# Two-layer encoder trunk on one core: another order of the transfers and small steps in the Fourier part that opens the kernel

## The chip, the cores and the metric

One Trainium2 chip, and one of its cores. The metric is the device time of one execution in microseconds (us), taken as the median of several runs; less is better. The profile describes one further execution, recorded by the hardware profiler.

## The reference, cut to what matters

Two inputs of 512 tokens by 1024 features, a prompt and a sample, go through the same two layers. Layer 0 mixes tokens with a two-dimensional Fourier transform, layer 1 with attention, and each is followed by a squared-ReLU MLP. All arithmetic is f32.

```python
def fourier_mix(h, w_out):
    B, S, _ = h.shape
    hg = h.astype(jnp.float32).reshape(B, S, N_FGROUPS, F_GROUP)
    f = jnp.fft.fft2(hg, axes=(1, 3), norm="ortho").real
    f = f.reshape(B, S, D_MODEL).astype(h.dtype)
    return f @ w_out
...
        if i % N_MIXERS == 0:
            x = x + fourier_mix(rms_norm(x, fourier_norm[j]), fourier_w_out[j])
        else:
            x = x + gqa_attention(rms_norm(x, attn_norm[j]), ...)
        x = x + sq_relu_mlp(rms_norm(x, mlp_norm[i]), mlp_w_up[i], mlp_w_down[i])
    return rms_norm(x, final_norm)
```

The features fall into 8 groups of 128, so the transform along the features is a product with a 128 by 128 table, and the one along the tokens a product with a 512 by 512 table.

## The kernel before, in words

The change touches only the Fourier part, which is about the first 6% of the span. It stands in one block under a manual schedule (L795 and after): each engine runs its instructions in the order in which the code issues them, so a step that waits holds up everything that the code puts behind it on that engine. TensorE is PE, VectorE DVE, ScalarE ACT, GpSimd POOL; SyncE (SP) only starts transfers.

**Sequences and tiles.** Sequence 0 is the prompt, sequence 1 the sample. Each has four tiles of 128 tokens. A `Front` object prepares two tiles of a sequence: `f0` and `f1` for sequence 0, `g0` and `g1` for sequence 1. It squares them on ACT (L130), forms the reciprocal root in six small steps (`chain`, L141 to L146, the second on ACT, the others on DVE), applies the gain (L429), and folds the 1024 features to their sum (`plus`, L433) and difference (`minus`, L442). For sequence 1 the sum is not made on DVE: `plus_there` (L438) has POOL start a transfer that adds one half of the tile onto the other while it is written (an accumulating transfer). `combine` (L464 to L489) joins the two tiles, `scale` (L453) brings them to the same root, and for sequence 1 the halves are split into two fp32r parts, high on ACT and low on DVE (L86, L87, L499, L504).

**The first product** is `transform_exact` (L643 to L668) for sequence 0: exact_even (L529), exact_odd (L532), exact_nyq (L535), then the feature products (L564, L585, L586). PE fills its waits there with a few idle products (`idle`, L604). Its results are split on ACT and DVE (L86, L87).

**The weights** of the output product are folded the same way by four `Fold` objects: `minus` (L684) makes the difference on DVE and then has POOL add the other half of the weight onto the first by an accumulating transfer (L685); odd_hi (L690) and even_hi (L702) are the high parts on ACT, odd_lo (L694) and even_lo (L705) the low parts on DVE.

**The second product** multiplies by these weights: eight odd outputs into the eight PSUM banks at once (`odd_outs`, L739), then the even ones (`even_outs`), each three products per part (L81, L82, L83) and one for the Nyquist rows (L745), whose weights POOL fetches (`FoldNyq.fetch`, L727). `odd_put` (L768, L769) and `even_put` (L777, L779) carry the banks to SBUF on ACT, which frees them. The residual input is added to the result by accumulating transfers of POOL (`add_input`, L792, one for each of the four tiles xs[0,0] to xs[0,3], 512 KB each), and the even part by two more on POOL for tiles 0 and 1 (`add_even`, L784) and on DVE for tiles 2 and 3 (L787, L789).

**Sequence 1** follows in `transform(1)` (L618 to L641): products with tables that POOL loads (dcos, dsin, dalt, dfeat; `table`, L329), evacuated by the splits of L86 and L87 one pair of banks after another. A hook called between them squares the finished tiles of sequence 0 for the next norm (`square`, L178 on ACT, then an addition on POOL, L182). Then `even_outs(1)` begins, and among its outputs stands the root of sequence 0 (`root`, L191, two columns per tile on PE), which reads the sum that POOL's last addition leaves. After it comes the spread of the root (L199), and the first MLP with its products (L1029).

**Loads.** SP starts the x tiles (L319), `load_xs(1)` (L168: the four residual tiles of sequence 1, 512 KB each), `put_away` (L212: a finished tile goes to DRAM, `park`), and the first MLP weights (`load_raw`, L101, 512 KB each). PSUM has 8 banks, each reused in order of the code; SBUF tiles of one kind share 38 slots, so a load can wait for a slot.

Of the kernel before, what the change touches and what calls it, by code (L numbers as in the profile page):

```python
# [16 lines left out]
ALU = mybir.AluOpType  # L17
# [27 lines left out]
def trunk_kernel(ctx, tc, x_in, xt_in, y_out, tables, rope, gfour, gcol, grow, gfin,  # L45
# [277 lines left out]
    def put_nyq():  # L323
        nyqs.append(slot([P, 512], F32R))
        nc.scalar.copy(nyqs[0], exact[2][:, 334:846])

    def table(k):
        tabs[k] = slot([P, D], F32R)
        nc.gpsimd.dma_start(tabs[k][:, : tables[k].shape[-1]], tables[k])  # L329
# [60 lines left out]
    def eights(x, n):  # L390
        return x[:, 0:512:64].unsqueeze(1).broadcast_to([P, n, 8])
# [14 lines left out]
    class Front:  # L406
# [52 lines left out]
        def low(self, i):  # L459
# [2 lines left out]
            nc.scalar.copy(self.n[i][:, :, 0], eights(self.m[i], 2))  # L462
            parts.append((self.p[i], self.m[i], self.n[i]))

        def combine(self):
            (p1, p2), (m1, m2), r, w = self.p, self.m, self.r, 8
            stt = nc.vector.scalar_tensor_tensor
            if self.q == 0:
                n, = nyq_tiles(1)
                stt(n[:, :, 0], eights(m2, 2), r[:, 1:2], eights(m1, 2), ALU.mult, ALU.add)  # L470
                stt(m2, m2, r[:, 1:2], m1, ALU.mult, ALU.subtract)
# [56 lines left out]
    def exact_even(k, j, o):  # L528
        nc.tensor.matmul(o[:, :258], parts[k][0][:, j * P : (j + 1) * P], cosX[k], start=k == 0, stop=k == 2)  # L529

    def exact_odd(k, j, v):
        nc.tensor.matmul(v[:, :256], parts[k][1][:, j * P : (j + 1) * P], sinX[k], start=k == 0, stop=k == 2)  # L532
# [67 lines left out]
    def idle(o, n, zero=None):  # L600

        w, alone = (filler, True) if zero is None else (zero, False)
        for _ in range(n):
            nc.tensor.matmul(o[:, :256], w, filler.unsqueeze(1).broadcast_to([P, 2, P]), start=alone, stop=alone)  # L604
# [35 lines left out]
        nyq_out(q, en)  # L640
        hook("feat", 3)  # L641

    def transform_exact(mid, hook):  # L643
        ov = [(ps(), ps()) for _ in range(4)]
        for k in range(2):
            for j in range(4):
                exact_even(k, j, ov[j][0])
            for j in range(4):
                exact_odd(k, j, ov[j][1])
        idle(ov[3][1], 9, an[:, :P])  # L650
        mid()
        ab = []
        for j in range(4):
            exact_odd(2, j, ov[j][1])
            exact_even(2, j, ov[j][0])
            ab.append(seq_evac(0, *ov[j]))
            hook("seq", j)
        on = ps()
        for k in range(3):
            exact_nyq(k, on)  # L660
        put_an(on)
        put_low(on)
        hook("an", 0)
        o = [feat_exact(*ab[j]) for j in range(2)]
        for j in range(4):
            feat_nyq(o[j][0], j)
            feat_split(0, j, *o[j])
            hook("feat", j)  # L668
            if 0 < j < 3:
                o.append(feat_exact(*ab[j + 1]))  # L670
# [80 lines left out]
    def odd_outs(q, fos):  # L751
        return outs(q, fos, wo, 256, 256)
# [42 lines left out]
    with tc.manual_schedule(engines={ET.PE, ET.Activation, ET.DVE, ET.Pool, ET.SP}):  # L795
# [29 lines left out]
        f0.root(1, 3, 4)  # L825
        f0.minus(1)
        f0.root(1, 4, 6)
        f0.table(1)
        f1.squares(1)
        f1.chain(1, 2)  # L830
        f0.low(0)
        f0.low(1)
        ftX = exact[2][:, :256]
        f1.gain(0)
        f1.minus(0)
        f1.gain(1)
        sums3 = []

        def mid():
            f1.chain(0, 1)  # L840
            f1.chain(2, 3)
            f1.plus(0)
            f1.chain(3, 4)
            f1.minus(1)
            f1.chain(4, 6)
            f1.scale()
            put_nyq()
            f1.plus(1)
            f1.combine()
            sums3.extend(odd_sums(k) for k in range(3))  # L850

        def hook0(at, j):
            if at == "seq":
                if j == 1:
                    for k in range(3):
                        put_sums(k, sums3[k])
                elif j == 3:
                    for f in fold:
                        f.minus()
                    fold[0].odd_hi()  # L860
            elif at == "an":
                fold[0].odd_lo()
# [11 lines left out]
        transform_exact(mid, hook0)  # L874
# [12 lines left out]
        g0.minus(0)  # L887
        g0.plus_there(0)
        for j in range(4):
            fold[j].even_hi()  # L890
        g0.chain(3, 4)
        fold[0].even_lo()
        g0.chain(4, 5)
        fold[1].even_lo()
        g0.chain(5, 6)
        fold[2].even_lo()
        fold[3].even_lo()
        for fo in range(2):
            odd_put(0, fo, o[fo])
        add_input(0, 0)  # L900
        g0.scale(slice(0, 1))
        for fo in range(2, 4):
            odd_put(0, fo, o[fo])
        add_input(0, 1)
# [10 lines left out]
        g1.squares(1)  # L915
        g1.chain(1, 2)
        for fo in range(6, 8):
            odd_put(0, fo, o[fo])
        g1.gain(1)
        g1.minus(1)  # L920
        g1.plus_there(1)
        for i in range(2, 4):
            add_input(0, i)

        def even(fo):
            even_put(0, fo, even_outs(0, [fo])[0])

        for fo in range(3):
            even(fo)
        g0.combine()  # L930
        g1.chain(0, 1)
        g1.chain(2, 3)
        add_even(0, 0)
        g0.split_even()
        g1.chain(3, 4)
        g0.split_odd()
        g1.chain(4, 6)
        even(3)
        g1.scale(slice(0, 1))
        g1.scale(slice(1, 2))  # L940
# [12 lines left out]
        blocks = Blocks(0)  # L953

        def hook1(at, j):
            if at == "seq":
                if j < 3:
                    square(0, j)
            else:
                square(0, 3 + j)  # L960
                if j == 3:
                    square(0, 7)

        transform(1, hook1)
        for fo in range(KC):
# [1244 lines left out]
```

## Time and profile before

| what | value |
|---|---|
| median of 3 runs | 1677.88 us (1676.66 to 1679.09) |
| the profiled execution's own time | 1676.81 us |
| its span in the trace | 1675.0 us, so 1.81 us lie around it |
| PE busy | 1662.4 us, 99% of the span |
| DVE, ACT, POOL busy | 76%, 52%, 23% |
| waits of PE listed with a releaser | 5.7 us in all, longest 1.2 us |
| the root of sequence 0 on PE (L191) begins | 74.06 us |

Times in a timeline count from the span's start. A row gives the start, the duration, the engine, the line, the operation and the tiles (result first), and in square brackets how long the engine stood idle before it and which event ended that. In a waits row stand the engine and its line, the event that it waited for, and then the us in total, the number of waits and the longest. A windows row gives for a stretch the busy time of PE, PE's weight loads, DVE, ACT and POOL, each with its count of instructions, then PE's granted clock, the mean busy share of the 16 DMA engines, and what they moved in GB/s.

### The profile page before, as it was taken

Reading aid. Unit: us, or ns where it says so; the run is one execution under the profiler, and the core shown is the slowest. Engines: PE = TensorE matmul, PEld = TensorE weight load, DVE = VectorE, ACT = ScalarE, POOL = GpSimd, SP = SyncE. Lnnn points to the kernel's source line nnn. Section 1 sums busy time; section 2 is a strip of 40 time slices with the busy share of each in tenths; the row PEclk is TensorE's granted clock in tenths of the full one; section 3 lists DMA queues with packets and bytes.
Section 4 is the critical chain, followed back from the end, with each engine's and each line's share of the span. In section 5 each row is a group of like instructions: output and inputs, shape, how many; then the busy total and the mean of one; then the engine's idle time right before and its main releaser. Section 6 shows DMA issues by size and latency. Waiting matters only on the chain.

```text
span 1675.0 us, 22279 instructions
## 1 busy us (share of the span) xinstructions
PE 1662.4 (99%) x7828; PEld 1386.3 (83%) x7828; DVE 1264.7 (76%) x1855; ACT 872.8 (52%) x1546; POOL 391.5 (23%) x370
## 2 busy tenths in 40 slices
PE   9999999999999999999999999999999999999998
PEld 8888888888888888888888888888888888888887
DVE  8679786557886869869888877777855487878875
ACT  7766444446343425446688855554454562433334
POOL 3321443221000001324444303004422220000002
PEclk9999999999999999999999999999999999999999
DMA  9942655449775757425501156334544695757632
GB/s 327 259 151 95 210 185 196 158 164 362 266 226 159 244 176 238 164 82 183 174 9 38 64 175 222 119 120 169 208 146 167 222 377 188 232 157 227 187 102 101
DMA packets 122480, 303.53 MB, mean 181 GB/s; under 512 B 12376, under 2 KB 13528, under 8 KB 122368
## 3 DMA queue, kind: packets, MB, share of 16 engines
q1 hardware_dynamic: 98720, 253.53, 43.7%
q0 software_dynamic: 9248, 22.10, 6.3%
q10 hardware_dynamic: 14400, 26.48, 4.2%
q8 instruction: 61, 1.00, 0.2%
q14 instruction: 51, 0.42, 0.1%
HBM read 217.59 MB, written 82.38 MB: 179 GB/s over the span
## 4 chain that ended last, share of the span: by engine, by line
PE 94%; DVE 2%; DMA 2%; ACT 1%; issue 0%; POOL 0%; SPq 0%; DVEq 0%; ACTq 0%; POOLq 0%
PE ps L1029 74%; PE ps L83 6%; PE ps L82 6%; PE ps L81 6%; PE ps L1624 2%; DMA u<-u 1%; DMA u<-spill_b 1%; PE ps L1603 0%; PE ps L191 0%; ACT u L86 0%; DVE u L429 0%; DMA u<-spill_t 0%; ACT w L702 0%; DVE u L87 0%; DVE t L442 0%
## 5 line engine op out<-in xcount | busy, mean ns | idle before, releaser
L1029 PE MATMUL ps<-u,w 128*128 128x512 f32 x4944 | 1131.0, 389 | 0.0
L1029 PEld LDWEIGHTS ps<-u,w 128*128 128x128 f32 x4944 | 926.4, 188 | 195.0 <-ACT u L1062 1.7
L86 ACT CAST w<-raw 128x1024 fp32r<-128x1024 f32 (+1 forms) x216 | 213.5, 994 | 309.8 <-PE ps L1029 238.4
L87 DVE TENSOR_TENSOR w<-raw,w 128x1024 fp32r<-128x1024 f32 (+1 forms) x216 | 251.4, 1167 | 75.4 <-ACT w L86 75.2
L86 ACT CAST u<-u 128x1024 fp32r<-128x1024 f32 (+1 forms) x140 | 140.7, 1046 | 85.3 <-PE ps L1029 37.9
L87 DVE TENSOR_TENSOR u<-u,u 128x1024 fp32r<-128x1024 f32 (+1 forms) x140 | 168.7, 1232 | 19.6 <-ACT u L86 19.1
L1029 PE MATMUL ps<-u,u 128*128 128x512 f32 x600 | 143.4, 389 | 0.5 <-DVE t L1239 0.5
L1239 DVE TENSOR_TENSOR u<-ps,u 128x512 f32<-128x512 f32 x160 | 109.4, 685 | 37.8 <-PE ps L1029 34.5
L1266 POOL DMA_DIRECT2D raw<-w_sum x32 | 27.7, 866 | 469.6 <-DVE w L87 164.7
L1147 POOL TENSOR_TENSOR u<-u 128x512 f32<-128x512 f32 x28 | 37.7, 1346 | 424.4 <-ACT u L1044 424.4
L1029 PEld LDWEIGHTS ps<-u,u 128*128 128x128 f32 x600 | 112.5, 188 | 24.6 <-DVE t L1239 0.9
L81 PE MATMUL ps<-u,u 128*128 128x512 f32 (+2 forms) x340 | 128.7, 381 | 1.2 <-ACT u L777 1.1
L82 PE MATMUL ps<-u,u 128*128 128x512 f32 (+2 forms) x340 | 124.1, 366 | 0.9 <-DVE u L87 0.9
L83 PE MATMUL ps<-u,u 128*128 128x512 f32 (+2 forms) x340 | 124.1, 366 | 0.2 <-DVE u L87 0.2
L182 POOL TENSOR_TENSOR t<-t,t 128x512 f32<-128x512 f32 (+1 forms) x54 | 79.2, 1471 | 191.9 <-ACT t L178 190.7
L1043 ACT ACTIVATE t<-t 128x512 f32<-128x512 f32 x64 | 40.5, 632 | 109.9 <-DVE t L1116 99.9
L83 PEld LDWEIGHTS ps<-u,u 128*128 128x128 f32 x340 | 64.2, 189 | 11.1 <-DVE u L87 0.7
L82 PEld LDWEIGHTS ps<-u,u 128*128 128x128 f32 x340 | 64.4, 189 | 10.3 <-DVE u L87 2.2
L87 DVE TENSOR_TENSOR u<-ps,u 128x512 fp32r<-128x512 f32 (+3 forms) x112 | 68.0, 634 | 6.3 <-ACT u L86 5.8
L81 PEld LDWEIGHTS ps<-u,u 128*128 128x128 f32 x340 | 64.4, 189 | 9.5 <-ACT u L777 1.4
L1103 DVE TENSOR_TENSOR t<-ps,u 128x512 f32<-128x512 f32 x32 | 22.0, 687 | 60.4 <-PE ps L1029 52.6
L178 ACT ACTIVATE t<-u 128x512 f32<-128x512 f32 (+1 forms) x64 | 38.1, 606 | 48.4 <-DVE u L1836 20.9
(282 smaller groups left out, 2043.4 us busy)
## 6 DMA issues: line engine op xcount, KB each, us to landing
raw<-w_up SPq DMA_DIRECT2D x80, 512.0 KB, 4.6
u<-spill_t SPq DMA_DIRECT2D x60, 512.0 KB, 6.9
raw<-w_sum SPq DMA_DIRECT2D x56, 512.0 KB, 5.4
u<-spill_b SPq DMA_DIRECT2D x45, 512.0 KB, 6.5
spill_t<-u SPq DMA_DIRECT2D x84, 256.0 KB, 2.0
spill_b<-t ACTq DMA_DIRECT2D x60, 256.0 KB, 4.3
raw<-w_row SPq DMA_DIRECT2D x28, 512.0 KB, 4.9
park<-u SPq DMA_DIRECT2D x24, 512.0 KB, 4.5
```

The source lines that it names most:

```text
L81: nc.tensor.matmul(out, lh, rh, start=first, stop=False)
L82: nc.tensor.matmul(out, lh, rl, start=False, stop=False)
L83: nc.tensor.matmul(out, ll, rh, start=False, stop=last)
L86: hi = nc.scalar.copy(dst_hi, src)
L87: return hi, eng.tensor_sub(dst_lo, src, f32(dst_hi))
L178: made = nc.scalar.activation(s[:, :n], xt(q, fo)[:, :n], AF.Square)
L182: nc.gpsimd.tensor_add(acc[q][:, :n], acc[q][:, :n], s[:, :n])
L1029: nc.tensor.matmul(o, w[x][:, sl], h[k][y], start=first and k + i == 0, stop=k == n - 1 and i == 2, skip_group_check=not first)
L1043: nc.scalar.activation(t, src, AF.Relu)
L1147: eng.tensor_sub(t[:, 0], b12, b11)
L1239: return nc.vector.tensor_add(x, o, x)
L1624: nc.tensor.transpose(pt[:, t * P : (t + 1) * P], probs[t][:, sc * P : (sc + 1) * P], ident)
```

## The change

Nothing is computed otherwise but one small sum (the Nyquist columns of `f1`, now formed after the difference has been overwritten). The rest is order:

- `f1`, tiles 2 and 3 of sequence 0: the root of both is formed ahead of tile 3's gain, the joined difference ahead of the sums, and `mid` is gone.
- `transform_exact`: one idle product fewer, and the last four odd products ahead of the last four even ones.
- The fourth weight fold's `minus`, with its accumulating transfer, goes from behind the third one to behind the second fold's low part.
- Sequence 1's first sum (`g0.plus_there(0)`) is asked for ahead of the Nyquist fetch and the four tables; the second and third ahead of most of the residual inputs, which are now added in the order 2, 0, 3, 1.
- The odd outputs come in the order 4, 5, 6, 7, 0 to 3 (tiles 2 and 3 first); the first two are put away between the weights' high parts, and `g0.scale` and `g1`'s squares stand behind the odd outputs.
- The first three even outputs are one group over three banks; the evacuation of even outputs 6 and 7 stands behind `g1`'s splits.
- The DVE addition for tile 3 (`add_even(0, 3)`) moves into the hook behind the first pair of sequence 1's evacuations.
- `load_xs(1)` is issued ahead of `put_away(0, 2)`.
- The squares of sequence 0 begin with tiles 2 and 3.

```diff
+        def combine_minus(self):
+            stt = nc.vector.scalar_tensor_tensor
+            stt(self.m[1], self.m[1], self.r[:, 1:2], self.m[0], ALU.mult, ALU.subtract)
...
-                stt(n[:, :, 0], eights(m2, 2), r[:, 1:2], eights(m1, 2), ALU.mult, ALU.add)
-                stt(m2, m2, r[:, 1:2], m1, ALU.mult, ALU.subtract)
                 stt(p1, p2, r[:, 1:2], p1, ALU.mult, ALU.add)
+                stt(n[:, :, 0], eights(m1, 2), 2.0, eights(m2, 2), ALU.mult, ALU.add)
...
-        idle(ov[3][1], 9, an[:, :P])
-        mid()
+        idle(ov[3][1], 8, an[:, :P])
         ab = []
         for j in range(4):
             exact_odd(2, j, ov[j][1])
+        for j in range(4):
             exact_even(2, j, ov[j][0])
...
                 elif j == 3:
-                    for f in fold:
+                    for f in fold[:3]:
                         f.minus()
-                    fold[0].odd_hi()
...
                 for t in range(2, NT):
                     behind(load_x(1, t), low, sync=True)
+                fold[3].minus()
                 fold[2].odd()
...
-        wn.fetch()
...
-        for k in range(4):
-            table(k)
-        o = odd_outs(0, range(KC))
+        order = [4, 5, 6, 7, 0, 1, 2, 3]
+        o = dict(zip(order, odd_outs(0, order)))
...
         g0.plus_there(0)
-        for j in range(4):
-            fold[j].even_hi()
+        wn.fetch()
+        for k in range(4):
+            table(k)
...
         g0.plus_there(1)
-        g0.scale(slice(1, 2))
-        g1.squares(0)
-        for fo in range(4, 6):
+        add_input(0, 2)
+        for fo in order[2:]:
             odd_put(0, fo, o[fo])
+        for i in range(2):
+            g0.scale(slice(i, i + 1))
         g1.gain(0)
         g1.minus(0)
         g1.plus_there(0)
...
+        e = even_outs(0, range(3))
...
         g1.plus_there(1)
-        for i in range(2, 4):
+        for i in (0, 3, 1):
             add_input(0, i)
...
-        for fo in range(4, KC):
+        for fo in range(4, 6):
             even(fo)
         g1.combine()
         g1.split_hi()
         g1.split_lo()
-        for i in range(2, 4):
-            add_even(0, i)
-
+        for fo in range(6, KC):
+            even(fo)
+        add_even(0, 2)
+
+        load_xs(1, xt_in[1])
         put_away(0, 2)
-        load_xs(1, xt_in[1])
...
                 if j < 3:
-                    square(0, j)
+                    square(0, order[j], first=4)
+                if j == 0:
+                    add_even(0, 3)
```

**POOL's transfers between the weight folds and the even parts.** The rows are POOL's, in order; u_449 to u_455 are the tables (u_559 to u_565 after), L727 (L730 after) is the Nyquist fetch, L438 the sums of sequence 1, and L792 (L795 after) the residual inputs, with u_441, u_443, u_445, u_447 the tiles 0 to 3 before and u_437, u_439, u_441, u_443 the same four after. Before:

```order
L727 DMA u_157<-nyq 8x1024 x3
...
L329 DMA u_449<-dcos 128x774
L329 DMA u_451<-dsin 128x1024
L329 DMA u_453<-dalt 128x594
L329 DMA u_455<-dfeat 128x512
L438 DMA u_562<-u_562 128x512
L792 DMA u_441<-xt 128x1024
L792 DMA u_443<-xt 128x1024
L438 DMA u_596<-u_596 128x512
L438 DMA u_608<-u_608 128x512
L438 DMA u_620<-u_620 128x512
L792 DMA u_445<-xt 128x1024
```

And now:

```order
L438 DMA u_550<-u_550 128x512
L730 DMA u_157<-nyq 8x1024 x3
L329 DMA u_559<-dcos 128x774
L329 DMA u_561<-dsin 128x1024
L329 DMA u_563<-dalt 128x594
L329 DMA u_565<-dfeat 128x512
L438 DMA u_588<-u_588 128x512
L795 DMA u_441<-xt 128x1024
L438 DMA u_608<-u_608 128x512
L438 DMA u_662<-u_662 128x512
L795 DMA u_437<-xt 128x1024
L795 DMA u_443<-xt 128x1024
```

The first sum has moved ahead of seven transfers, the second ahead of two inputs, and the inputs of tiles 0, 3 and 1 stand behind all four sums. The two L784 transfers of the even parts (L787 after) stay last.

**SP's transfers behind the x tiles.** L319 is an x tile, L212 the parking of tile 2 of sequence 0, L168 the residual tiles of sequence 1, L101 the first MLP weights. Before:

```order
L319 DMA u_417<-x 128x1024
L319 DMA u_419<-x 128x1024
L212 DMA park<-u_445 128x1024
L168 DMA u_795<-xt 128x1024
L168 DMA u_797<-xt 128x1024
L168 DMA u_799<-xt 128x1024
L168 DMA u_801<-xt 128x1024
L101 DMA raw_803<-w_up 128x1024
```

And now:

```order
L319 DMA u_414<-x 128x1024
L319 DMA u_416<-x 128x1024
L168 DMA u_791<-xt 128x1024
L168 DMA u_793<-xt 128x1024
L168 DMA u_795<-xt 128x1024
L168 DMA u_797<-xt 128x1024
L212 DMA park<-u_441 128x1024
L101 DMA raw_800<-w_up 128x1024
```

The four loads no longer stand behind a store that needs the finished tile 2.

**DVE around the weight folds.** L684 (L687 after) makes the difference of a fold, which its accumulating transfer waits for; L608 and L614 (L611 and L617 after) split the Nyquist sums, L694 (L697 after) is the low part of an odd weight, L87 (eight rows, of which only the last is shown) the low part of the features. Before:

```order
L684 TENSOR_TENSOR u_233<-raw_232,u_233 128x1024
L684 TENSOR_TENSOR u_237<-u_236,u_237 128x1024
L608 TENSOR_TENSOR u_95<-ps_364,u_95 8x258
L614 SCALAR_TENSOR_TENSOR u_97<-ps_364,u_97 24x258
L694 TENSOR_TENSOR u_362<-u_223,u_361 128x1024
...
L87 TENSOR_TENSOR u_408<-ps_404,u_408 128x255
L694 TENSOR_TENSOR u_414<-u_229,u_413 128x1024
L694 TENSOR_TENSOR u_422<-u_233,u_421 128x1024
```

And now:

```order
L687 TENSOR_TENSOR u_233<-raw_232,u_233 128x1024
L611 TENSOR_TENSOR u_95<-ps_358,u_95 8x258
L617 SCALAR_TENSOR_TENSOR u_97<-ps_358,u_97 24x258
L697 TENSOR_TENSOR u_367<-u_223,u_366 128x1024
...
L87 TENSOR_TENSOR u_405<-ps_401,u_405 128x255
L697 TENSOR_TENSOR u_411<-u_229,u_410 128x1024
L687 TENSOR_TENSOR u_237<-u_236,u_237 128x1024
L697 TENSOR_TENSOR u_421<-u_233,u_420 128x1024
```

The fourth difference (u_237) went from ahead of the Nyquist split to behind the second fold's low part, twelve rows later.

More of the change, by code (lines that the diff above doesn't have):

```diff
@@ L834, in trunk_kernel @@
         f1.gain(0)
+        f1.chain(0, 1)
+        f1.chain(2, 3)
         f1.minus(0)
+        f1.chain(3, 6)
+        f1.scale(slice(0, 1))
         f1.gain(1)
[L837 to L850, printed above, removed]
+        f1.minus(1)
+        f1.combine_minus()
+        f1.plus(0)
+        f1.scale(slice(1, 2))
+        put_nyq()
+        f1.plus(1)
+        f1.combine()
+        sums3 = [odd_sums(k) for k in range(3)]
         def hook0(at, j):
             if at == "seq":
-                if j == 1:
+                if j == 0:
                     for k in range(3):
@@ L888, in trunk_kernel @@
         g0.plus_there(0)
[L889 to L890 removed]
+        wn.fetch()
+        for k in range(4):
+            table(k)
         g0.chain(3, 4)
+        fold[0].even_hi()
         fold[0].even_lo()
         g0.chain(4, 5)
+        fold[1].even_hi()
         fold[1].even_lo()
         g0.chain(5, 6)
[L896 to L898 removed]
+        for fo in order[:2]:
             odd_put(0, fo, o[fo])
[L900 to L904, printed above, removed]
+        for j in range(2, 4):
+            fold[j].even_hi()
+            fold[j].even_lo()
         g0.gain(1)
@@ L914, in trunk_kernel @@
         g1.plus_there(0)
[L915 to L918, printed above, removed]
+        e = even_outs(0, range(3))
+        for fo in range(2):
+            even_put(0, fo, e[fo])
+        g1.squares(0)
         g1.gain(1)
@@ L921, in trunk_kernel @@
         g1.plus_there(1)
-        for i in range(2, 4):
+        for i in (0, 3, 1):
             add_input(0, i)
+        even_put(0, 2, e[2])
+        g1.squares(1)
+        g1.chain(1, 2)
         def even(fo):
             even_put(0, fo, even_outs(0, [fo])[0])
-        for fo in range(3):
-            even(fo)
         g0.combine()
@@ L933, in trunk_kernel @@
         add_even(0, 0)
+        even(3)
         g0.split_even()
@@ L937, in trunk_kernel @@
         g1.chain(4, 6)
-        even(3)
-        g1.scale(slice(0, 1))
-        g1.scale(slice(1, 2))
         add_even(0, 1)
-        for fo in range(4, KC):
+        for i in range(2):
+            g1.scale(slice(i, i + 1))
+        for fo in range(4, 6):
             even(fo)
@@ L957, in hook1 @@
                 if j < 3:
-                    square(0, j)
+                    square(0, order[j], first=4)
+                if j == 0:
+                    add_even(0, 3)
             else:
-                square(0, 3 + j)
+                square(0, order[3 + j], first=4)
                 if j == 3:
-                    square(0, 7)
+                    square(0, order[7], first=4)
         transform(1, hook1)
```

8 lines of the change are left out of this document (4 added, 4 removed).

## The prediction, as put on record before the run

> **What bounds the kernel now.** I read the page first, then the waits of PE, then the chain that ended last.
>
> ```profile
> span 1675.0 us, 22279 instructions
> PE 1662.4 (99%) x7828; PEld 1386.3 (83%) x7828; DVE 1264.7 (76%) x1855; ACT 872.8 (52%) x1546; POOL 391.5 (23%) x370
> PE ps L81 <- ACT u L777: 1.1, 1, 1.1
> PE ps L532 <- DVE t L471: 1.0, 1, 1.0
> PE ps L82 <- DVE u L87: 0.9, 1, 0.9
> PE ps L81 <- ACT u L769: 0.4, 1, 0.4
> PE ps L83 <- DVE u L87: 0.2, 1, 0.2
> 118.61 588.02 PE ps L1029 x2592
> ```
>
> PE is busy 99% of the span, and in the last line, a piece of the chain, it works 588 us from 118.61 us on without a gap. So the whole kernel is a string of products, and what the change does to the time is by how much PE reaches the MLP earlier or later; nothing behind 118 us can give it back. The waits say what there is to win: the five lie in the stretch that is reordered, and sum to 1.1 + 1.0 + 0.9 + 0.4 + 0.2 = 3.6 us. Removing all of them would be a gain of 0.21%, while there is no such lid on a loss. I count as "the same" what lies within 0.2%, 3.4 us, about what a measurement of this kernel can tell from no change.
>
> Then the windows, for the transfers (the last two numbers of a row are the DMA share and the GB/s):
>
> ```profile
> 45.00:50.00 5.00, 4.61 (x39) 4.41 (x38) 0.99 (x4) 4.97 (x18) 1.71 (x2) 1.00 1.05 195
> 55.00:60.00 5.00, 4.39 (x34) 4.19 (x35) 4.45 (x8) 3.65 (x11) 0.86 (x1) 1.00 1.05 202
> 65.00:70.00 5.00, 4.92 (x37) 4.34 (x35) 3.48 (x10) 5.00 (x16) 3.94 (x5) 1.00 1.02 419
> 43.95 6.07 DMA u<-u
> 56.42 8.26 DMA u<-u
> ```
>
> The DMA engines are full in all three. From 45 to 60 us they move some 200 GB/s, when POOL's accumulating transfers run; from 65 to 70, when SP's plain loads run alone, 419. So 512 KB cost 0.524 MB / 0.2 = 2.6 us of all 16 engines when accumulated and 0.524 / 0.419 = 1.25 us when loaded. The last two rows are from the chain: two accumulating transfers stand on it, the second sum of sequence 1 and the last even part. That is the real limit of this stretch: **a full DMA system**, of which PE's waits are the far end.
>
> **The change, part by part.**
>
> *First product and folds (to 40 us).* DVE, lines L684, L608 and L705:
>
> ```profile
> 22.90 1.22 DVE L684 TENSOR_TENSOR u<-u,u 128x1024 f32<-128x1024 f32 x1
> 24.15 0.42 DVE L608 TENSOR_TENSOR u<-ps,u 8x258 fp32r<-8x258 f32 x1
> 38.94 1.22 DVE w L705
> 28.16 0.86 POOL L685 DMA_DIRECT2D u<-w_four  x1 [3.95 <-DVE u L87]
> u<-w_four POOLq DMA_DIRECT2D x1, 512.0 KB, 7.5
> 33.48 3.79 ACT w L702 x4
> ```
>
> With the fourth L684 moved, the Nyquist split can begin up to 1.22 us earlier, and the 1.0 us wait at L532 can shrink with the earlier join. But DVE does the same work up to the last L705, which ends at 40.16 and is in the chain, and the even products need it: I price the gain at 0 (bounds -1.0, the whole wait, and 0). The moved L684 starts behind one L694, near 30.7 us, so its transfer is asked for near 31.5 instead of 28.16, and by the 7.5 us of the row less some queue that is gone it lands near 37.7 instead of 35.7. The fourth L702 cast (the last quarter of the 3.79 us) needs it, and two odd outputs' evacuations stand around it. Third bank: first two casts and two evacuations to about 37.7 us, two casts to 39.6, the third evacuation to 40.2; the group of three even outputs wants it after two quarter passes, near 39.2 + 0.7 = 39.9, or up to 1.1 us before it comes. I take **+1.0** (bounds 0 and +1.1). In exchange the 0.4 us wait on L769 goes: no evacuation stands behind this row any more.
>
> ```profile
> 43.66 0.72 ACT L453 ACTIVATE u<-u,s 128x512 f32<-128x512 f32 x1 [3.60 <-DMA u<-u]
> 36.44 0.90 POOL L438 DMA_DIRECT2D u<-u  x1 [2.18 <-DVE w L705]
> 31.25 0.84 POOL L329 DMA_DIRECT2D u<-dsin  x1
> u<-x SPq DMA_DIRECT2D x1, 512.0 KB, 7.6
> u<-x SPq DMA_DIRECT2D x1, 512.0 KB, 9.7
> ```
>
> *POOL's queue.* ACT stood idle 3.6 us for the first sum, which is why it was put ahead. But its L438 began at 36.44 after 2.18 us of waiting for DVE: **it is held by its data, not by the queue**, and with the same DVE work ahead it will again begin at 36.5 to 37. Now the Nyquist fetch and the four tables wait behind it, though they had no reason to: dsin, issued at 31.25, goes to about 39.5. POOL's queue then has little to move from 33 to 37. The two x loads, which landed 7.6 and 9.7 us after 30.7 and 31.1, get that time and land sooner; the rest of POOL's work, tables and sums, I put 2.8 us later than before (tables' issue 8 us later, less the 2.5 us of the x loads and the time in which the sum would have queued anyhow; bounds 1 and 4).
>
> *The sums of g1 (52 to 58 us).*
>
> ```profile
> 49.04 0.85 POOL L438 DMA_DIRECT2D u<-u  x1 [1.75 <-ACT u L769]
> 55.21 1.18 ACT L777 COPY u<-ps 128x257 f32<-128x257 f32 x4
> u<-u POOLq DMA_DIRECT2D x1, 256.0 KB, 3.5
> ```
>
> The last sum is issued at 49.04 and lands 3.5 us later, at 52.5. Behind the two inputs less and the first residual load more it will land near 54.8 (bounds 52 and 56). From there: two scales of 0.7 us, one join of 0.75, two splits of 0.65, and now behind these the evacuation of even output 6, which frees a bank of sequence 1's first product. Before, four evacuations freed it at 56.4. 54.8 + 0.7 + 0.75 + 2 x 0.6 = 57.5: **+1.1** at this point for the 1.1 us wait on L777, which therefore doubles instead of going away (bounds -1.1 and +2.2).
>
> *The residual loads (SP).*
>
> ```profile
> 59.62 0.33 SPq L212 DMA_DIRECT2D park<-u  x1
> 60.01 4.45 SPq L168 DMA_DIRECT2D u<-xt  x4
> 51.62 0.89 POOL L792 DMA_DIRECT2D u<-xt  x1 [0.44 <-issue]
> u<-xt POOLq DMA_DIRECT2D x1, 512.0 KB, 7.7
> 52.90 0.87 POOL L784 DMA_DIRECT2D u<-u  x1 [0.38 <-issue]
> u<-u POOLq DMA_DIRECT2D x1, 512.0 KB, 9.0
> ```
>
> Before, the four L168 loads stood behind the parking store, at 60.01, when the accumulating transfers were nearly done. Now nothing holds them but a free slot, which the first gets near 47 us and the others when the last even products release theirs, near 52. So 4 x 1.25 = **5.0 us of full DMA time enters a queue that is full already**, in front of or beside tile 3's input (issued 51.62, landed 59.3) and the first even part (issued 52.90, landed 61.9). Nobody needs these loads before the residual of sequence 1, behind the point where L191 stands. What they cost depends on how loads share with accumulating transfers. Nearest rows: the two x loads, 2.5 us of full DMA time, got through from about 33 to 40.8 us beside POOL's work, a third of the time. I take a third.
>
> Tile 3's input is now the eighth of POOL's sums instead of seventh and lands, without the loads, near 60.8; with a third of 8 us, 2.6 us, near 63.4. Then DVE's addition (1.21 + 0.16 us) and, behind it on DVE, the next pair of splits (0.43 + 0.41): they end near 65.1, where they ended at 63.6 before, and the bank for sequence 1's last tile comes with them, some 1.7 us after its time: **+1.8** at this point (bounds -0.9 and +4). The 0.9 us wait at L82, which DVE's two additions made, goes, and this one comes in its place. Queued behind that DVE step is also the rest of sequence 1's splits, so all products after it move.
>
> *The squares and the root (65 to 78 us).*
>
> ```profile
> 64.78 0.63 ACT L178 ACTIVATE t<-u 128x512 f32<-128x512 f32 x1 [0.59 <-DMA u<-u]
> 67.41 0.68 ACT L178 ACTIVATE t<-u 128x512 f32<-128x512 f32 x1
> 68.59 5.40 POOL L182 TENSOR_TENSOR t<-t,t 128x512 f32<-128x512 f32 x4 [0.37 <-ACT u L86]
> 74.06 0.37 PE L191 MATMUL ps<-ones,t 128*128 128x2 f32 x2
> ```
>
> The first even part lands 9.0 us after 52.90, at 61.9. Now: +2.8 for POOL's later queue, +1.3 for the wait of the second sum on its data, +5.0 for the loads served by then, at 71.0. Tiles 2 and 3 are squared first, which puts its square fifth; the fifth began at 67.41, with the 1.8 of delay 69.2, so ACT waits 1.8 us there, its next casts stand behind it, and PE behind these: **+3.6**. The last even part follows by 2.6 us and half as much again for parking and the first MLP weights, which now wait beside it, near 74.9. Two squares and two of POOL's additions (5.40 / 4 = 1.35 us) end at 74.9 + 0.6 + 2.7 = 78.2, and the root can begin: 78.2 against 74.06, **+4.2** (bounds -0.5 and +8.7).
>
> The steps are not added up: each is the delay of PE at its place, and the last one covers the ones before. Behind L191 the order is the old one. So the profiled execution's own time of 1676.81 us becomes 1681.0, and the median, 1.07 above it (1677.88), **1682.1 us**.
>
> **A rule against a row.**
>
> ```profile
> 34.00:35.00 1.00, 1.00 (x10) 1.00 (x10) 1.00 (x3) 1.00 (x2) 0.26 (x1) 1.00 0.95 333
> 61.00:62.00 1.00, 0.28 (x2) 0.28 (x3) 0.96 (x3) 0.05 (x1) 0.00 (x0) 1.00 1.03 205
> 62.00:63.00 1.00, 1.00 (x11) 1.00 (x10) 0.12 (x1) 1.00 (x3) 0.00 (x0) 1.00 1.05 221
> ```
>
> With the store and the first load asked for at 59.6 and 60.0, the stretch from 61 to 62 still moves 205 GB/s, the rate of accumulating transfers alone: no load got through for two us. Read strictly, loads give way until the sums are done, and then the change costs little. The Trainium skill, "DMA: Bandwidth & Descriptors", section "Queues, rings and completion order", says otherwise: an engine goes round the queues that have work, a packet at a time. By that rule the loads take their turns as soon as they have arrived, and the time is near the forecast; by the row it is that of the first rival. The 333 GB/s from 34 to 35 us, a mixture, agree with the rule.
>
> **The rivals.**
>
> *Loads give way.* For it speaks the row at 61 us; against it 333 GB/s at 34. Then tile 3's input lands near 60.8 and the even parts near 66 and 69.7, before they are wanted. What stays is the +1.1 at g1's sums: 1676.81 + 1.0 = 1677.8, median 1678.9, **not slower** by the bound. It decides from here: tile 3's input before 62 us and the first even part before 69.
>
> *Loads take half or more.* For it: at 34 us, (333 - 200) / (419 - 200) = 0.6 of the time went to loads. Against: there the others were largely tables, not accumulating. The first even part then lands at 75.6 and the last near 79.5, so L191 at 82.8: +8.7, 1685.5, median 1686.6.
>
> *The waits go.* If the third bank, the sums and tile 3's input all come in time, the waits of 1.1, 0.9, 0.4 and 0.2 vanish: -2.6, median 1675.3; with the one at L532, -3.6 and 1674.3. Against it is that L438 is held by DVE.
>
> **How the numbers follow.** Forecast 0.48, loads give way 0.27, half or more 0.17, waits go 0.08. Slower by over 0.2% are the third case and the forecast but for its lower edge, 0.61; faster by as much only the end of the last, 0.05; the same 0.34. The range reaches over the first rival to 1677.0 and into the second to 1687.0. The forecast's own is 1680.5 to 1685.
>
> **What would show it.** In the profile after: L168 issued between 46 and 53 us and 250 to 300 GB/s from 50 to 65; the first L438 still near 37, dsin at 39 or later; a wait of PE on an evacuation near 41, one of some 2 us on ACT's L780 near 57, one on DVE's L87 near 65, and ACT's L178 idle for a DMA near 71; L191 near 78. I am wrong if L178 finds its tile there, or if windows with loads asked for stay at 200 GB/s.

## The result, and the profile after

The changed kernel takes **1684.75 us** (median of 6 runs, 1683.8 to 1687.35) against 1677.78 us before (6 runs): a ratio of 1.0046, 95% interval 1.0033 to 1.0059. It is slower by 7.0 us between the medians, and by 7.7 us by the ratio, by which the runs below are compared. That is beyond the 0.2% that a measurement can tell apart, and inside the range of the prediction, which had put it at 1682.1. The span in the trace grew from 1675.0 to 1682.0 us.

The waits of PE in the changed kernel (engine and line, what it waited for, us in total, times, longest):

```profile
PE ps L81 <- ACT u L780: 4.0, 2, 2.4
PE ps L81 <- DVE u L87: 2.6, 2, 2.0
PE ps L81 <- ACT u L86: 1.7, 1, 1.7
PE ps L81 <- ACT u L772: 0.9, 1, 0.9
PE ps L532 <- ACT u L457: 0.4, 1, 0.4
PE ps L191 <- POOL t L182: 0.3, 1, 0.3
```

They sum to 9.9 us, where the five of before summed to 3.6. Only the wait at L532 shrank, from 1.0 to 0.4, and for the 0.4 us at L769 there are 0.9 at L772. The others grew: the banks behind the even outputs (L780, L777 before) cost 4.0 for 1.1, in two waits that end at 55.34 and 58.73 us, and the splits of sequence 1 (L87) 2.0 for 1.1; the other 0.6 of the 2.6 stands at 26.7 us, in sequence 0.

The chain that ended last shows whose far end these waits are (start, us, what):

```profile
54.59 11.47 DMA u<-xt
66.08 1.22 DVE u L790
70.50 8.22 DMA u<-u
78.81 0.64 ACT t L178
126.83 587.99 PE ps L1032 x2592
```

Tile 3's input travels for 11.5 us, 7.7 before; then the last even part from 70.50 to 78.7, which had been asked for at 56.42 and had landed at 64.7. The MLP's unbroken stretch begins at 126.83 instead of 118.61, **8.2 us later**, and the root (L191) at 82.27 instead of 74.06, the same 8.2. So the whole loss is made ahead of the root.

POOL's transfers, which the next rows explain (start, duration, line, and in brackets POOL's wait ahead of it):

```profile
36.73 0.86 POOL L438 DMA_DIRECT2D u<-u  x1 [3.87 <-DVE s L144]
39.36 0.87 POOL L329 DMA_DIRECT2D u<-dsin  x1
...
54.59 0.86 POOL L795 DMA_DIRECT2D u<-xt  x1 [0.91 <-issue]
56.54 0.89 POOL L795 DMA_DIRECT2D u<-xt  x1 [1.09 <-ACT ny L86]
62.89 0.87 POOL L787 DMA_DIRECT2D u<-u  x1 [5.46 <-ACT t L178]
70.50 0.86 POOL L787 DMA_DIRECT2D u<-u  x1 [6.74 <-ACT u L86]
```

The first sum begins at 36.73, held by DVE as it was at 36.44 before, and dsin goes from 31.25 to 39.36. The two last rows are what the prediction had not named. POOL stands for 5.5 and 6.7 us ahead of the even parts, and asks for them **10 and 14 us later** than before (52.90 and 56.42). The events in the brackets are not what it waits for: ACT's copies that these transfers read were done by 49.2 us. An even part is added into the same tile as its input, and the inputs of tiles 0 and 1 now stand just ahead of it: tile 0's landed 9.4 us after 52.81, at 62.24, tile 1's 13.3 us after 56.54, at 69.85, and each even part follows 0.65 us behind. The second tells most: from 66.1, when tile 3's input had landed, only two of POOL's transfers were under way, where three often are, and still it waited for tile 1's.

SP's loads and the DMA system in four windows (the last three numbers are PE's clock, the DMA share and GB/s):

```profile
46.24 6.97 SPq L168 DMA_DIRECT2D u<-xt  x4
```

```profile
56.00:57.00 1.00, 0.31 (x3) 0.10 (x1) 0.67 (x1) 0.00 (x0) 0.46 (x1) 1.00 1.07 406
58.00:59.00 1.00, 0.27 (x2) 0.28 (x3) 1.00 (x2) 0.95 (x3) 0.00 (x0) 1.00 1.01 254
61.00:62.00 1.00, 1.00 (x7) 1.00 (x6) 0.42 (x1) 0.62 (x2) 0.00 (x0) 0.50 1.02 221
65.00:66.00 1.00, 0.75 (x7) 0.54 (x5) 0.00 (x0) 0.00 (x0) 0.00 (x0) 1.00 1.06 283
```

The residual loads are asked for from 46 to 53 us, as foreseen, and run beside the sums. At 406 GB/s they have the DMA engines nearly to themselves: POOL's next input had been issued at 52.81, and its first packet, by its 4 KB, begins at 56.88. At 254 and 283 both queues run, at 65 with the parking store and the first MLP weights in the place of the loads, of which the last landed at 64.15. And PE's clock stands at 0.50 at 61, which it did in no window of before from 30 to 84 us.

Not all of the 8.2 us reaches the end. At L199 in layer 1 the lag is still 1076.03 - 1067.86 = 8.2 us, at L1971 (L1974) 1648.48 - 1641.49 = 7.0. Between them the chain of the kernel before leaves PE for two reloads from DRAM:

```profile
1498.63 5.24 DMA u<-spill_t
...
1511.75 8.39 DMA u<-spill_b
```

In the changed kernel the same stretch is one piece of PE (550.04 us from 1076.47). 1.2 us came back there, where the prediction held that nothing could; the cause, some 1400 us behind the change, stays open.

### The profile page after: what moved, and what is told of

Same layout as the page of the kernel before. It is cut to its first block, busy times and chain, and to the rows that moved or that the text cites. A ratio compares the mean times of both kernels' runs of the same rounds, so it can differ in the third digit from the quotient of the medians.

```text
span 1682.0 us, 22285 instructions
## 1 busy us (share of the span) xinstructions
PE 1663.5 (99%) x7827; PEld 1388.8 (83%) x7827; DVE 1263.9 (75%) x1855; ACT 873.9 (52%) x1546; POOL 392.4 (23%) x370
## 4 chain that ended last, share of the span: by engine, by line
PE 94%; DVE 2%; DMA 1%; ACT 1%; issue 1%; POOL 0%; DVEq 0%; POOLq 0%; ACTq 0%
PE ps L1032 75%; PE ps L81 5%; PE ps L83 5%; PE ps L82 5%; PE ps L1627 2%; DMA u<-xt 1%; DVE u L429 1%; DMA u<-u 0%; PE ps L1606 0%; PE ps L191 0%; DVE t L442 0%; DVE u L687 0%; ACT u L86 0%; PE ps L607 0%; ACT u L693 0%
## 5 line engine op out<-in xcount | busy, mean ns | idle before, releaser
L87 DVE TENSOR_TENSOR w<-raw,w 128x1024 fp32r<-128x1024 f32 (+1 forms) x216 | 251.4, 1167 | 75.5 <-ACT w L86 75.2
L87 DVE TENSOR_TENSOR u<-u,u 128x1024 fp32r<-128x1024 f32 (+1 forms) x140 | 168.8, 1234 | 16.4 <-ACT u L86 15.9
L82 PE MATMUL ps<-u,u 128*128 128x512 f32 (+2 forms) x340 | 124.3, 367 | 0.0
L1046 ACT ACTIVATE t<-t 128x512 f32<-128x512 f32 x64 | 40.5, 632 | 111.1 <-DVE t L1119 101.1
L87 DVE TENSOR_TENSOR u<-ps,u 128x512 fp32r<-128x512 f32 (+3 forms) x112 | 67.9, 634 | 7.8 <-ACT u L86 7.2
L83 PEld LDWEIGHTS ps<-u,u 128*128 128x128 f32 x340 | 64.7, 190 | 10.5 <-DVE u L87 0.3
L82 PEld LDWEIGHTS ps<-u,u 128*128 128x128 f32 x340 | 64.9, 191 | 8.6 <-DVE u L87 0.3
```

Of the source, the lines that this page charges most:

```text
L82: nc.tensor.matmul(out, lh, rl, start=False, stop=False)
L83: nc.tensor.matmul(out, ll, rh, start=False, stop=last)
L87: return hi, eng.tensor_sub(dst_lo, src, f32(dst_hi))
L1046: nc.scalar.activation(t, src, AF.Relu)
```

## The experiments

Theory A, the prediction's: the residual loads, ahead of their store, fill a DMA system that is full. Rival B: POOL's own order, the first sum ahead of the tables. Rival C: PE's clock. Each run was compared with the kernel before on the same chip; differences in us are the ratio's share of 1677.6 us. Theories D, F and G came with the results. Where a profile shows a wait of PE of 0.3 to 0.6 us for the very first load (L358), which the first two profiles lack, its times stand up to 1 us later throughout, so the times are compared by medians.

**1. Loads back behind the store, all else changed.**

```diff
-        load_xs(1, xt_in[1])
         put_away(0, 2)
+        load_xs(1, xt_in[1])
```

> The changed kernel with one step undone: the four residual loads of sequence 1 are issued behind the parking store again, as before. Theory A (the loads fill a full DMA system): tile 3's input lands near 61 us instead of 66.1, the even parts near 66 and 70 instead of 73.7 and 78.7, the root of sequence 0 (L191) begins near 75 instead of 82.3, and the time falls by 6 to 7 us to 1677 to 1679, within 0.2% of before. Rival B (POOL's own order: the first sum and what waits behind it, the fourth fold): the inputs stay late, L191 stays at 80 or later and the time falls by less than 2 us. Rival C (PE's clock, which falls to 0.50 after the waits, makes the delay): the time falls only as far as the waits do, and the windows at 60 to 63 us stay at 0.50 in either case.

Measured: 1683.14 us, ratio 1.0029 (1.0019 to 1.0039). Still 4.9 us slower than before: A as the whole fails. Waits of PE, and from the chain:

```profile
PE ps L191 <- POOL t L182: 4.0, 1, 4.0
```

```profile
64.38 11.12 DMA u<-u
```

PE's waits ahead are short now (1.5, 0.9 and 0.6 us on L780, L772 and L87), but the root waits 4.0 us for the last even part, asked for only at 64.38 and 11.1 us on the way. By then the loads, though in their old place, run beside it.

**2. The loads alone, on the kernel before.**

```diff
-        put_away(0, 2)
         load_xs(1, xt_in[1])
+        put_away(0, 2)
```

> The kernel before with this one step alone: the four residual loads ahead of the parking store. Theory A: nearly the whole loss appears without any other part of the change: the even part of tile 0, squared first here, lands near 67 instead of 61.9, L191 begins 5 to 7 us later than 74.1, and the time is 5 to 7 us longer. Rival B: the loads alone cost under 2 us, since POOL's sums are in their old places.

Measured: 1683.74 us, ratio 1.0037 (1.0023 to 1.005), 6.2 us slower. From the waits and from the chain:

```profile
PE ps L82 <- DVE u L87: 2.3, 1, 2.3
```

```profile
58.98 13.26 DMA u<-u
```

The last even part takes 13.3 us instead of 8.3. So A alone makes most of the loss, and by run 1 most of it is also there without A.

**3 and 4. Tables ahead of the first sum again**, in the changed kernel (3), and with the loads back as well (4).

```diff
-        g0.plus_there(0)
         wn.fetch()
         for k in range(4):
             table(k)
+        g0.plus_there(0)
```

> The changed kernel with POOL's fetch and four tables ahead of the first sum again, as before, all else changed. Rival B: POOL's queue is filled from 33 to 37 us again, its later transfers come 2 to 3 us sooner, and the time falls by 2 to 3 us. Theory A: what POOL gains there the loads take away later; the time falls by under 1.5 us, and waits of several us stay at 54 to 59, 66 and 73 us.

> Both undone: residual loads behind the parking store and POOL's tables ahead of the first sum, all else changed. Theory A with B as a smaller part: L191 near 74 to 75, time at or up to 1 us under that of the loads alone put back. If A is the whole, equal to it within 0.5 us.

Measured: 1685.11 us, 1.0046 (1.0031 to 1.006), for 3; 1682.71 us, 1.0032 (1.0019 to 1.0045), for 4. Neither differs from its neighbour (changed kernel, run 1). B falls: with the rest of the change in place, the tables' 8 us of delay cost nothing that can be measured, nor does the first sum's place. Run 5, which leaves both as the change has them, lies 1.2 us above the kernel before by its ratio, so little is left for them.

**5 and 6. The inputs of tiles 0 and 1 early again**, with the loads back (5) and with the loads ahead (6). Theory D: an even part waits for its own tile's input.

```diff
         g0.plus_there(1)
-        add_input(0, 2)
         for fo in order[2:]:
             odd_put(0, fo, o[fo])
+        for i in range(2):
+            add_input(0, i)
...
-        for i in (0, 3, 1):
+        for i in range(2, 4):
             add_input(0, i)
```

> The changed kernel with two steps undone: the residual loads behind the parking store, and the inputs of tiles 0 and 1 asked for behind the second sum and ahead of the sums of g1, tiles 2 and 3 behind them, as in the kernel before. Theory D (an even part goes into the same tile as its input, so POOL cannot ask for it before that input has landed; with the inputs of tiles 0 and 1 last, the even parts were asked for 10 and 14 us later than before, into the time of the loads): the even parts are issued near 53 and 57 us and land by 66, POOL's wait of 4 us at L191 is gone, L191 begins near 75 and the time is within 2 us of before, 1677 to 1680. Rival A+ (the loads were all, and what remains comes from another part, such as the fourth fold or the evacuations): L191 stays near 79 and the time near 1683.

> The changed kernel with only the inputs of tiles 0 and 1 early again, the loads still ahead of the store. Theory D with A: the loads alone still take 4 to 6 us, as they did in the kernel before: L191 near 79, time 1682 to 1684. If D were all: L191 near 75, time near 1678.

Measured: 5 takes 1679.02 us, ratio 1.0007 (0.9998 to 1.0017); 6 takes 1682.83 us, 1.0031 (1.002 to 1.0042). With both undone the loss is gone but for 1.2 us, and the interval holds no difference too; with one of them it is 5. In run 5 POOL asks for the even parts thus:

```profile
57.97 0.87 POOL L787 DMA_DIRECT2D u<-u  x1 [0.92 <-ACT ny L86]
60.84 0.86 POOL L787 DMA_DIRECT2D u<-u  x1 [2.00 <-ACT u L780]
```

That is 5 and 10 us sooner than in the changed kernel, if later than the 53 and 57 expected, and the root waits for POOL no more. In run 6 it does not wait for POOL either. There the loads run beside the last sum of sequence 1, which is on its way from 53.56 to 61.94 us, and PE waits for the banks that are freed behind it:

```profile
PE ps L81 <- ACT u L780: 7.9, 2, 5.1
```

**7. Late inputs alone, on the kernel before.**

```diff
-        add_input(0, 0)
...
-        add_input(0, 1)
...
-        for i in range(2, 4):
+        for i in (2, 0, 3, 1):
             add_input(0, i)
```

> The kernel before with one step alone: the four residual inputs asked for behind the last sum of g1, in the order 2, 0, 3, 1. Theory D: the even parts are issued several us later (59 and 65 instead of 52.9 and 56.4), run beside the loads, and the time is 3 to 6 us longer although no load was moved. If D is wrong: within 1 us of before.

Measured: 1685.25 us, ratio 1.0042 (1.0025 to 1.0059), 7.0 us slower with no load moved. POOL's even parts, and PE's waits:

```profile
58.30 0.87 POOL L784 DMA_DIRECT2D u<-u  x1 [2.63 <-ACT u L499]
63.21 0.86 POOL L784 DMA_DIRECT2D u<-u  x1 [4.04 <-issue]
```

```profile
PE ps L81 <- DVE u L87: 6.2, 3, 3.1
```

```profile
65.68 0.63 ACT L178 ACTIVATE t<-u 128x512 f32<-128x512 f32 x1 [5.97 <-DMA u<-u]
74.02 0.63 ACT L178 ACTIVATE t<-u 128x512 f32<-128x512 f32 x1 [6.11 <-DMA u<-u]
```

That is more than the 3 to 6 us expected. What holds PE is the even parts: ACT squares tiles 0 and 1 first here and waits 6.0 and 6.1 us for them, and the splits that PE's banks need stand behind. The even parts follow the landings of their own tiles' inputs (57.64 and 62.56 us) by 0.66 and 0.65 us, as in the changed kernel (0.65 both) and in run 1 (0.65 and 0.66).

D holds, from both sides. The two causes are one collision reached from two sides: **the loads moved into the time of the even parts, or the even parts into the time of the loads**; run 6 shows that the loads, moved, also run into the last sum of sequence 1.

Ratios of 1.0037 and 1.0042 alone make 1.0046 together, although the delays of the last even part nearly add up: it lands at 64.67 us before, and 7.6 us later in run 2, 9.3 in run 7 and 14.1 in the changed kernel. The order of the squares fits the difference. Where tiles 0 and 1 are squared first (before, runs 2 and 7), the root begins 9.4 to 9.8 us behind that landing; in the changed kernel and in run 1, which square them last, 3.5 to 3.6 us.

**8. The first product alone**, on the kernel before: `combine_minus`, the early chain of f1, eight idle products, odd products first (the first three pieces of the diff, and the steps of `f1` that go with them).

> The kernel before with only the part up to 24 us changed: the early root and joined difference of f1, one idle product fewer, odd products ahead of even ones. By the prediction's step it gains 0 (0 to 1 us): DVE's order up to the last low part of the weights is as long as before. If the wait at L532 was on the path, 1 us faster.

Measured: 1678.15 us, ratio 1.0004 (0.9994 to 1.0013). No gain, as priced: PE's wait at L532 is 0.3 us there instead of 1.0, but one of 0.7 us came at L567 behind it.

**9. Idle products in run 5's waits.** Theory F: the clock's fall costs time. Run 5's PE waited 2.0 and 2.3 us on bank evacuations, and then:

```profile
PE ps L81 <- ACT u L780: 4.3, 2, 2.3
```

```profile
57.13 0.28 PE L82 MATMUL ps<-u,u 128*128 128x256 f32 x1
57.25 0.29 PE L83 MATMUL ps<-u,u 128*128 128x256 f32 x1
...
62.46 0.42 PE L81 MATMUL ps<-u,u 128*128 128x258 f32 x1
62.68 0.42 PE L82 MATMUL ps<-u,u 128*128 128x258 f32 x1
```

```profile
63.00:64.00 1.00, 1.00 (x7) 1.00 (x7) 0.34 (x2) 0.39 (x2) 0.00 (x0) 0.50 1.07 213
```

Products follow each other every 0.12 us ahead of the second wait and every 0.22 behind it, at a granted clock of 0.50. The edit adds work that computes nothing, into a bank that the next product starts anew.

```diff
     def seq_part(q, j, c, o, v):
+        if q == 1 and c == 0 and 0 < j < 3:
+            idle(o, 12 + 2 * j)
```

> As e5 (loads back, inputs of tiles 0 and 1 early), with 14 and 16 idle products put into PE's two waits near 55 and 58 us, which they nearly fill (1.7 of 2.0 us and 1.9 of 2.3 us). Theory F (the clock's fall to 0.50 after those waits costs time of its own: 21 products at 0.215 instead of 0.12 us, 2.0 to 2.4 us): the clock stays at 1.00 from 58 to 65 us, L191 begins 2 us earlier than in e5 and the time is 1.5 to 2.5 us under that of e5, at or under 1677.5. Rival (the landings behind set the end in any case): the clock stays up, but L191 and the time are within 0.7 us of e5.

Measured: 1677.58 us, ratio 1.0005 (0.9996 to 1.0014). The idle products and the clock in the same stretch:

```profile
53.88 1.84 PE L609 MATMUL ps<-u 128*128 128x256 f32 x14
57.64 2.08 PE L609 MATMUL ps<-u 128*128 128x256 f32 x16
```

```profile
58.00:59.00 1.00, 1.00 (x11) 1.00 (x10) 0.92 (x2) 0.13 (x1) 0.71 (x1) 1.00 1.00 197
60.00:65.00 5.00, 4.61 (x39) 4.52 (x39) 4.78 (x11) 3.75 (x12) 1.12 (x2) 1.00 1.05 206
```

The clock stays at 1.00, and the root begins at 75.05 instead of 76.83. In the profile F holds, with 1.8 us. The times do not settle it: the medians are 1.4 us apart, the ratios 0.3, and each interval is 0.1% wide either way.

**10. Evacuations of even outputs 6 and 7 ahead of g1's splits**, on run 5.

```diff
-        for fo in range(4, 6):
+        for fo in range(4, KC):
             even(fo)
         g1.combine()
         g1.split_hi()
         g1.split_lo()
-        for fo in range(6, KC):
-            even(fo)
```

> As e5, with the evacuations of even outputs 6 and 7 ahead of g1's splits again, as in the kernel before. The step priced at 1.1 us in the prediction: PE's two waits on these evacuations, 4.3 us in e5, fall to about 1 to 1.5 us, the clock stays at 1.00, and the time is 2 to 4 us under e5, at 1675 to 1677. If the order of ACT here is not what holds the bank: waits and time as in e5.

Measured: 1676.99 us, ratio 0.9997 (0.9988 to 1.0006), against 1.0007 in run 5. The wait that remains on that line:

```profile
PE ps L81 <- ACT u L780: 1.6, 1, 1.6
```

4.3 became 1.6 us, so ACT's order does hold the bank. But a wait of 1.9 us on L87 came behind it, with the clock at 0.66 on the mean from 65 to 70 us, and the root begins at 76.86, as in run 5 (76.83). By the ratios there are 1.7 us in it, by the profile none, and the intervals overlap: what the step is worth stays open.

**11. The squares alone**, tiles 2 and 3 first, on the kernel before.

```diff
-                    square(0, j)
+                    square(0, 4 + j, first=4)
...
-                square(0, 3 + j)
+                square(0, (7 + j) % 8, first=4)
```

> The kernel before with only the squares of sequence 0 in the new order, tiles 2 and 3 first. ACT's wait of 2.76 us for the even part of tile 0 at 61.95 goes, and with it PE's wait of 0.9 us at L82 and DVE's waits behind it: 0.5 to 1.2 us faster, 1676.5 to 1677. If the even parts, squared last, then hold the root: L191 no earlier and the time within 0.3 us of before.

Measured: **1675.83 us, ratio 0.999 (0.9981 to 0.9999)**: the one part that makes the kernel faster than before, by 1.7 us, if only just clear of the interval's end. ACT's first square:

```profile
60.73 0.63 ACT L178 ACTIVATE t<-u 128x512 f32<-128x512 f32 x1 [0.39 <-DVE u L789]
```

It waited 2.76 us before, for the even part of tile 0. But the wait on L82 that was to go with it stayed (1.0 us), so the gain came behind it, not by the step expected: PE ends that wait at 62.98 us, 1.3 later than before, and begins the root at 73.64, 0.4 sooner. Small gaps between PE's products, behind the squares and casts, are what went.

**12. Idle products in the changed kernel's waits** (the edit of run 9).

> The changed kernel itself with 14 and 16 idle products in PE's waits of 1.55 and 2.41 us on the bank evacuations at 55 to 59 us. Theory G (in the changed kernel the fall of the clock to 0.50 at 60 to 63 us costs nothing of its own, since PE waits again for tile 3's input at 66 and for the even parts at 73 to 79): the clock stays at 1.00 at 60 to 63, the wait at 67 grows by 1.5 us or so, L191 and the time stay within 0.7 us of the changed kernel, 1684 to 1685.5. Rival C (the clock is a term of the loss): 1.5 to 2 us faster, under 1683.3.

Measured: 1685.18 us, ratio 1.0047 (1.0033 to 1.006): no gain. The clock is 1.00 over 60 to 65:

```profile
60.00:65.00 5.00, 4.40 (x37) 4.19 (x36) 1.42 (x4) 3.24 (x9) 0.87 (x1) 1.00 1.08 278
```

PE then waits for tile 3's input (2.1 us) and the even parts all the same. The wait did not grow as expected; the input landed 1.3 us earlier in this execution's time. C falls for the changed kernel: its first fall of the clock lies ahead of later waits. The second, from 76.8 to 80.2 us, these idle products do not reach (76.3 to 79.7 here); behind it the root waits for POOL in both kernels (0.3 and 0.6 us), so PE was not the later one.

## Why the prediction was right, and where it was short

**Right.** The sign, and the reasoning that a full DMA system bounds this stretch. The third bank: a wait of 0.9 us for 1.0 forecast. The first sum: 36.7 for 36.5 to 37, dsin at 39.4 for 39.5. The 0 for the first product (run 8). The bank behind g1's splits: PE resumed at 58.73, 57.5 forecast; what was missing was 1.4 us in the last sum's landing, 56.2 (7.2 us after 48.98) for 54.8. The wait of 1.55 us ahead of it was not forecast: there ACT's scale waits for the third sum, which lands at 54.28, and the first of these evacuations stands behind it.

**The step that was short** is the landing of the inputs and even parts: tile 3's input at 66.1 for 63.4, the even parts at 73.7 and 78.7 for 71.0 and 74.9, the root at 82.3 for 78.2, so 8.2 us for 4.2. Two sums of the forecast are off by little, and not the cause: the splits behind tile 3's input end at 63.4 + 1.21 + 0.16 + 0.43 + 0.41 = 65.6 by its own terms, not 65.1, and 78.2 - 74.06 is 4.1. Two things were missing in it.

First, "a third" for the loads. The trace counts packets, MB and share of the 16 engines by queue, POOL's q0 and SP's q1. From 58 to 59 us, and then from 65 to 66:

```profile
q0 software_dynamic: 30, 0.12, 64.3%
q1 hardware_dynamic: 33, 0.13, 36.8%
```

```profile
q0 software_dynamic: 34, 0.14, 67.5%
q1 hardware_dynamic: 36, 0.15, 38.8%
```

SP's queue had 36.8 / 101.1 = 0.36 of the DMA time, and 0.37 the second time, so a third holds **where both queues have work**. By the Trainium skill, "DMA: Bandwidth & Descriptors", section "Queues, rings and completion order", queues take turns packet by packet, and these windows agree: 30 packets against 33, and 34 against 36. A load's packet costs half of an accumulated one (0.18 and 0.34 us for 4 KB from 58 to 59 us). But at 56 us, at 406 GB/s, the loads had nearly everything. What POOL had moving was done by 56.23, and the next, tile 0's input, issued at 52.81, moved nothing until 56.88.

Second, the wait of an even part for its own tile's input. The prediction treated the even parts as held by the DMA queue alone; POOL waited 5.5 and 6.7 us for landings. Run 7 shows that this alone costs 7.0 us.

**The terms that were not terms**: +2.8 us for the tables behind the first sum (runs 3 and 4: nothing measurable). The forecast's sum came near by them, so a near size was partly luck: the loads' share and the unnamed wait were each worth the whole.

**The rivals.** "Loads give way" fails by the 254 GB/s at 58 us, with 0.36 of the DMA time for SP's queue; the row at 61 us of before, on which it rested, could not show it: SP's queue, asked for the store at 59.62, began no packet before 62.74. "Half or more" is nearest in time, but by a late start of POOL's transfers, not by a larger share. "The waits go" needed inputs in time; run 11 shows that 1.7 us of it was to be had by the squares' order alone.

## What to carry to other kernels

A load that nobody is waiting for is not free when the DMA engines are full: ask which transfer with a waiting reader it will run beside, and keep it behind that one's issue. When accumulating transfers into one tile are reordered, write down for each which earlier landing it must wait for; the queue's order hides this wait until the first of the pair is moved back. The times of parts that meet at one place need not add up, so undo them in pairs as well as one by one, and try each alone: here one good part of 1.7 us lay under two that cost 6 and 7.

## What the runs showed of the hardware

- **Under load a transfer's first packet can come 2 to 4 us after it was asked for.** SP's queue in the kernel before, asked for the store at 59.62 and the first load at 60.01, began its first packet at 62.74 us; the first residual load after the change, asked for at 46.24, began at 48.35, and tile 0's input, asked for at 52.81, at 56.88 (told by its 4 KB packets; those of the sums ahead of it are 2 KB). It is not always so late: the two x loads after the change, asked for from 30.03 us on, began at 31.18. What sets the delay stays open.
- **With three accumulating transfers under way, POOL asked for the next 0.31 us after one had landed.** After the change it asked at 52.81, 54.59 and 56.54, behind landings at 52.50, 54.28 and 56.23; before, at 51.62, 52.90 and 56.42, behind 51.31, 52.59 and 56.11.
- **PE's clock fell to half for 3.41 us, or two or three times that.** In the changed kernel it was 0.50 from 59.71 to 63.12 and from 76.78 to 80.19 us, in run 5 from 58.06 to 64.89, in run 6 from 58.25 to 68.49. How long PE waits does not settle it alone: a wait of 1.9 us in run 10 was followed by 0.50 from 66.14 to 69.55, while one of 2.0 us at 66 in the changed kernel did not lower it. The Trainium skill, "TensorE: Matmul & The Clock Gate", Part 1, has such a gate with two states, full and half, set by how busy PE was in a window of about 3.4 us; the 0.50 and 1.00 of these rows and their 3.41 us agree. The 30 idle products of run 9, of 0.12 us each, kept the clock at 1.00.
